# Strassen's seven block products for the second product of a two-layer transformer's MLPs on one Trainium2 core

## The chip, the core and the metric

The kernel runs on one core of a Trainium2 chip. The metric is the device time of one execution in microseconds, as the median of several runs. Five engines matter: TensorE (PE) multiplies matrices, with its weight loads shown apart (PEld); VectorE (DVE) and ScalarE (ACT) do elementwise work and can read the accumulators in PSUM; GpSimd (POOL) does elementwise work on SBUF; SyncE (SP) only issues the DMA loads here. Each engine takes its instructions in the order in which they were issued to it, and they meet at semaphores.

## The reference

Two layers over 256 tokens with a model width of 1024. Layer 0 mixes tokens by block-sparse attention, which with 256 tokens is causal attention over one block; layer 1 by dilated windows. After each mixer comes an MLP with 4096 hidden units:

```python
def sq_relu_mlp(x, w_in, w_out):
    return jnp.square(jax.nn.relu(x @ w_in)) @ w_out

for i in range(DEPTH):
    ...
    h = layer_norm(DEEPNORM_ALPHA * h + mix, ln_mix_g[i], ln_mix_b[i])
    h = layer_norm(DEEPNORM_ALPHA * h + sq_relu_mlp(h, mlp_w_in[i], mlp_w_out[i]),
                   ln_mlp_g[i], ln_mlp_b[i])
```

All is float32. The second product, `... @ w_out`, is 256 x 4096 by 4096 x 1024; it is the one that the change touches.

## The kernel before

**Precision.** PE multiplies in float32r, a rounded form of float32. To keep float32's accuracy each operand is split into a high part (`hi`, rounded) and the rest (`lo`), and a product is three matmuls: hi·hi, hi·lo and lo·hi. ACT makes `hi` with a copy (line 309), DVE makes `lo` by subtracting `hi` from the source (line 314); that pair is `split`. For a weight tile from memory (`load_w`) it is 1024 columns: one load of 512 KB into one of four `raw` buffers, one ACT copy into `whi`, one DVE subtraction into `wlo`, each with ten slots.

**The MLP.** The 4096 hidden units are 32 k-tiles of 128. The first four are computed token-major (`half`, `relu_sq_tok`), with the normalised tokens stationary, since the first half of the tokens is ready before the second; they are then transposed on PE. The other 28 are computed one at a time with a tile of W_in stationary (`mm_wstat_wide`): eight matmuls of 512 columns, which take tokens' hi and lo side by side, and eight of 256 for the weight's lo. `relu_sq_T` takes the result out of its PSUM bank (tag `tp`): an ACT copy of one half, a DVE add of the other, a DVE instruction for relu and square, and a split into `ahi` and `alo`. Four k-tiles after they were made, `do_out` multiplies them by W_out: for each k-tile, two halves of the tokens (m), two halves of the columns (n) and three matmuls, 12 of 512 columns (`mm_rows`, line 318). Four accumulators (tag `acc`) hold the sums; `tp` has four banks, `acc` four, eight in all. The last `TAIL` k-tiles are ordered by accumulator and not by k-tile (`out_and_ln`), so that the first half's normalisation (`ln_half`) starts while the second half still accumulates.

**Order.** All work is first recorded as operations with an engine, an assumed duration and the buffers that they read and write (`Plan.op`). `Plan.order` then simulates the engines with these durations, with slots for each buffer tag, and gives each engine one fixed order by due times; `emit` issues it. An addition on POOL is assumed to take n/480 + 0.17 us (`tt`). POOL has the addition in `rotate` (line 514, 28 times, SBUF to SBUF, 256 elements) and one instruction for each `rstd` of a normalisation (line 699). SP's queue holds all loads in program order.

Of the kernel before, what the change touches and what calls it, by code (L numbers as in the profile page):

```python
# [12 lines left out]
P = 128  # L13
S = 256
# [10 lines left out]
SCALE = HD ** -0.5  # L25
NEG = -1.0e30
BIG = 3.0e38
NCH = DFF // 512
NX = (1, 1)
TAIL = (5, 5, 6, 8)  # L30
NSLOT = 10
ADD_ENG = "POOL"
ORDER0 = (
# [215 lines left out]
def tile_trunk(  # L249
# [42 lines left out]
    def psum(tag):  # L292
        return mk([P, 512], F32, tag, 4, ps_pool)
# [13 lines left out]
    def split(n, src, hi, lo, r, whi, wlo, sbuf=False, hi_eng="ACT"):  # L307
        if hi_eng == "ACT":
            op("ACT", act(n, sbuf=sbuf), lambda: nc.scalar.activation(hi(), src(), AF.Copy), r, whi)  # L309
        else:  # L310
            op("DVE", dve(n), lambda: nc.vector.tensor_copy(hi(), src()), r, whi)
        op(
            "DVE", dve(n),
            lambda: nc.vector.tensor_tensor(lo(), src(), f32(hi()), op=ALU.subtract), list(r) + list(whi), wlo,  # L314
        )

    def mm(out_ap, lhsT, rhs, start, stop):
        nc.tensor.matmul(out_ap, lhsT, rhs, start=start, stop=stop)  # L318
# [115 lines left out]
    def load_gb(i):  # L434
        return load_row(i, lng, "g"), load_row(i, lnb, "b")
# [54 lines left out]
                )  # L490

    def mm_rows(pieces, item, m):
        (ahi, alo, j), w, pos, total = item
        first, last = pos == 0, pos == total - 1
        t = slice(m * P, (m + 1) * P)

        def go():
            a, b = ahi.t[:, j, t], alo.t[:, j, t]
            for acc, c0, n in pieces:
                mm(acc.t[:, :n], a, w.hi.t[:, c0 : c0 + n], first, False)  # L500
                mm(acc.t[:, :n], a, w.lo.t[:, c0 : c0 + n], False, False)
            for acc, c0, n in pieces:
                mm(acc.t[:, :n], b, w.hi.t[:, c0 : c0 + n], False, last)

        op(
            "PE", 3 * sum(n / 2400 + 0.0135 for _, _, n in pieces), go,
            [(w.hi, 0), (w.lo, 0), (ahi, (j, m)), (alo, (j, m))], [acc for acc, _, _ in pieces],
        )
# [7 lines left out]
    def stt(n, aps, dst, a, s, b, o0, o1, r, w):  # L516
        op(
            "DVE", dve(n, aps),
            lambda: nc.vector.scalar_tensor_tensor(dst(), a(), s(), b(), op0=o0, op1=o1), r, w,  # L519
        )  # L520
# [155 lines left out]
    def act_tiles():  # L676
        return mk([P, 4, S], F32R, "ahi", 3), mk([P, 4, S], F32R, "alo", 3)

    def ln_half(pieces, m, gb, last, ahead):
        g, b = gb  # L680
        z = xtok[m]
        step = min(n for _, _, n in pieces)
# [4 lines left out]
        ns = D // step  # L687
        for acc, c0, n in pieces:
            c = slice(c0, c0 + n)
            stt(n, 0, lambda c=c: z.t[:, c], lambda c=c: z.t[:, c], lambda: ALPHA, lambda acc=acc, n=n: acc.t[:, :n],  # L690
                ALU.mult, ALU.add, [(z, c0 // 512), acc] + prev, [(z, c0 // 512)])
            for i in range(c0 // step, (c0 + n) // step):
                op("DVE", dve(step), lambda i=i: nc.vector.bn_stats(st.t[:, i, :], z.t[:, i * step : (i + 1) * step]),  # L693
                   [(z, c0 // 512)], [(st, i)])
                prev = [(st, i)]
# [29 lines left out]
                    [(xs[n], (1, *k)) for k in keys],  # L725
                )

    def new_acc(last=False):
        acc = [[(psum("acc"), n * 512, 512) for n in range(2)] for _ in range(2)]
        if last:  # L730
            acc[1] = [acc[1][0], (acc[1][1][0], 512, 256), (psum("tp"), 768, 256)]
        return acc

    def out_and_ln(acc, items, ntail, gb, last, between):
        k = len(items) - ntail
        for item in items[:k]:
            for m in range(2):
                mm_rows(acc[m], item, m)
        for m in range(2):
            for piece in acc[m]:  # L740
                for item in items[k:]:
                    mm_rows([piece], item, m)
            if m == 1 and between:
                between()
            ln_half(acc[m], m, gb, last, 1.5 if m == 1 and between else 0.0)

    def relu_sq_T(ps, ahi, alo, j):
        u = mk([P, S], F32, "ta", 5)
# [7 lines left out]
            [(ahi, k) for k in keys], [(alo, k) for k in keys], sbuf=True,  # L756
        )

    def relu_sq_tok(ps, m, ahi, alo):
        r = mk([P, 512], F32, "hrt", 1)  # L760
        op("ACT", act(512), lambda: nc.scalar.activation(r.t, ps.t, AF.Relu), [ps], [r])  # L761
        op("ACT", act(512, 0, True), lambda: nc.scalar.activation(r.t, r.t, AF.Square), [r], [r])
        pt = psum("tp")
        transposes(pt, [(j * P, lambda j=j: r.t[:, j * P : (j + 1) * P]) for j in range(4)], [r])
        t = slice(m * P, (m + 1) * P)
        keys = [(j, m) for j in range(4)]
        split(
            512, lambda: pt.t.rearrange("p (j s) -> p j s", j=4), lambda: ahi.t[:, :, t], lambda: alo.t[:, :, t],
            [pt], [(ahi, k) for k in keys], [(alo, k) for k in keys],
        )  # L770

    class Mlp:
        def __init__(self, i, last):
            self.i, self.last = i, last
            self.nx = NX[i]

        def head(self):
            i, nx = self.i, self.nx
            self.ws = [[load_w(win[i][c * 4 + j]) for j in range(4)] for c in range(nx)]
            self.chunks = {c: act_tiles() for c in range(nx)}  # L780
            self.half(0)

        def half(self, m):
            ps = [psum("tp") for _ in range(self.nx)]
            for c in range(self.nx):
                mm_xstat(ps[c], self.ws[c], m, 512, "x")
            for c in range(self.nx):
                relu_sq_tok(ps[c], m, *self.chunks[c])

        def rest(self, between):  # L790
            i, nx, chunks = self.i, self.nx, self.chunks
            self.half(1)
            acc = new_acc(self.last)
            nkt = DFF // P
            ntail = TAIL[2 * i + 1]
            pend = list(range(nx))
            tail = []

            def do_out(c):
                for j in range(4):  # L800
                    pos = c * 4 + j
                    item = ((*chunks[c], j), load_w(wout[i][pos]), pos, nkt)
                    if nkt - pos <= ntail:
                        tail.append(item)
                    else:
                        for m in range(2):
                            mm_rows(acc[m], item, m)

            for c in range(nx, NCH):
                if c == 4:  # L810
                    gb = load_gb(2 * i + 1)
                    if i == 0:
                        ropes.append(const(rope1, [P, 2, S], "ropet"))
                        late["m1"] = const(mask1, [P, 2, 512], "m1")
                chunks[c] = act_tiles()
                for j in range(4):
                    w = load_w(win[i][c * 4 + j])
                    ps = psum("tp")
                    mm_wstat_wide(ps, w)
                    relu_sq_T(ps, *chunks[c], j)  # L820
                pend.append(c)
                while len(pend) > 1:
                    do_out(pend.pop(0))
            while pend:
                do_out(pend.pop(0))
            out_and_ln(acc, tail, len(tail), gb, self.last, between)

    def layer0(between):
        attn = [act_tiles() for _ in range(2)]
# [53 lines left out]
        for step, p in (x.split("-") for x in ORDER0.split()):  # L883
# [13 lines left out]
                sm[p] = softmax(q, k)  # L897
            else:
                pv_causal(*sm.pop(p), V[p // 4], (p % 4) * P, *attn[p // 4], p % 4)
        items = [((*attn[j // 4], j % 4), load_w(wo0[j]), j, 8) for j in range(8)]  # L900
# [18 lines left out]
    def layer1(between):  # L919
# [4 lines left out]
        for step, a in (x.split("-") for x in ORDER1.split()):  # L924
# [49 lines left out]
            else:  # L974
# [8 lines left out]
        items = [((*attn[j // 3], j % 3), load_w(wo1[j]), j, 6) for j in range(6)]  # L983
        out_and_ln(new_acc(), items, TAIL[2], gb, False, between)

    mlps = [Mlp(0, False), Mlp(1, True)]
# [14 lines left out]
def _layout(inputs):  # L1001
# [34 lines left out]
    wi = []  # L1036
    for i in range(DEPTH):
        t = a["mlp_w_in"][i]
        k = NX[i] * 512
        parts = ([wide_tiles(t[:, :k], 512)] if k else []) + [col_tiles(t[:, k:])]  # L1040
        wi.append(np.concatenate(parts))
# [57 lines left out]
```

## Time and profile before

| | us |
|---|---|
| median of 3 runs (577.32 to 578.2) | 577.36 |
| profiled execution | 577.73 |
| its span | 576.0 |
| MLP of layer 0 with its neighbours, stretch 135 to 310 | 175 |
| MLP of layer 1, stretch 395 to 560 | 165 |
| DMA in all | 105.61 MB, 183 GB/s over the span |

The span goes from the first to the last instruction that the profiler recorded, the time from start to end of the execution. Busy shares count an engine's instructions from start to end. Matmuls overlap in a pipeline, so their mean duration (379 ns for 512 columns) is longer than the step from one to the next; steps are read from the chain or from counts in a stretch. An instruction that waits within the engine for something shows as a longer one and not as idle time.

### The profile page before, as it was taken

How to read it: one execution, taken by the hardware profiler on the slowest of the kernel's cores; microseconds unless marked ns; L12 is line 12 of the kernel's file. 1: busy time of each engine (PE TensorE's matmuls, PEld its weight loads, DVE VectorE, ACT ScalarE, POOL GpSimd, SP SyncE). 2: the span in 40 equal slices, each digit the busy share in tenths (PEclk: the TensorE clock that was granted, in tenths of full speed). 3: DMA queues.
4: the chain of work that ended last, by engine and by line, in shares of the span. 5: the costliest groups of instructions: out<-in, count | busy, mean ns of one | idle time of the engine just before them, and what ended most of it. 6: DMA issues, size and time to landing. Idle time of an engine off the chain costs nothing.

```text
span 576.0 us, 8655 instructions
## 1 busy us (share of the span) xinstructions
PE 563.0 (98%) x3234; PEld 486.9 (85%) x3234; DVE 430.1 (75%) x771; ACT 300.5 (52%) x501; POOL 40.4 (7%) x41
## 2 busy tenths in 40 slices
PE   8899999999999999999999999999999999999994
PEld 7799898788888888888888999878888888888884
DVE  5799989798874775665768899978876756756544
ACT  6585677636753554454525455754764544544400
POOL 0211121010000000000000323000000000000000
PEclk9899999999999999999999999999999999999998
DMA  8644943726986875565524533544888655655101
GB/s 303 236 151 151 326 130 123 221 74 220 304 261 220 258 215 185 184 205 181 197 75 158 207 112 111 172 157 129 279 279 263 202 196 172 200 184 182 36 1 73
DMA packets 30281, 105.61 MB, mean 183 GB/s; under 512 B 3488, under 2 KB 4256, under 8 KB 30240
## 3 DMA queue, kind: packets, MB, share of 16 engines
q1 hardware_dynamic: 30240, 105.07, 56.0%
q8 instruction: 25, 0.41, 0.3%
q14 instruction: 16, 0.13, 0.1%
HBM read 104.01 MB, written 1.05 MB: 182 GB/s over the span
## 4 chain that ended last, share of the span: by engine, by line
PE 95%; DVE 1%; DMA 1%; ACT 1%; issue 0%; POOL 0%; SPq 0%; DVEq 0%
PE acc L318 55%; PE tp L318 38%; PE tp L598 2%; DMA raw<-in_xw_dram 1%; DVE ta L512 0%; DVE tok L519 0%; POOL ta L514 0%; ACT xs L309 0%; ACT hrt L761 0%; DVE wlo L314 0%; SPq L305 0%; ACT whi L309 0%; ACT khi L540 0%; DVE klo L519 0%; DVE bst L693 0%
## 5 line engine op out<-in xcount | busy, mean ns | idle before, releaser
L314 DVE TENSOR_TENSOR wlo<-raw,whi 128x1024 fp32r<-128x1024 f32 (+2 forms) x185 | 225.6, 1226 | 74.1 <-ACT whi L309 73.0
L309 ACT ACTIVATE whi<-raw 128x1024 fp32r<-128x1024 f32 (+2 forms) x184 | 191.3, 1046 | 129.6 <-PE tp L318 57.1
L318 PE MATMUL acc<-whi,ahi 128*128 128x512 f32 (+1 forms) x312 | 119.6, 383 | 0.0
L318 PE MATMUL acc<-wlo,ahi 128*128 128x512 f32 (+1 forms) x312 | 117.3, 380 | 0.0
L318 PE MATMUL tp<-xs,whi 128*128 128x512 f32 x448 | 112.0, 392 | 0.0
L318 PE MATMUL acc<-whi,alo 128*128 128x512 f32 (+1 forms) x312 | 100.7, 379 | 0.0
L318 PEld LDWEIGHTS tp<-xs,whi 128*128 128x128 f32 x448 | 81.1, 189 | 14.9
L318 PEld LDWEIGHTS acc<-whi,ahi 128*128 128x128 f32 x312 | 58.7, 188 | 11.3 <-issue 0.9
L318 PEld LDWEIGHTS acc<-wlo,ahi 128*128 128x128 f32 x312 | 58.7, 188 | 10.4
L318 PE MATMUL acc<-xs,whi 128*128 128x256 f32 x448 | 64.9, 288 | 1.5 <-ACT whi L309 1.5
L318 PEld LDWEIGHTS acc<-whi,alo 128*128 128x128 f32 x312 | 57.1, 188 | 10.4
L318 PEld LDWEIGHTS tp<-xs,wlo 128*128 128x128 f32 x448 | 61.0, 190 | 4.2
L318 PE MATMUL tp<-xs,wlo 128*128 128x256 f32 x448 | 62.6, 283 | 0.0
L318 PEld LDWEIGHTS acc<-xs,whi 128*128 128x128 f32 x448 | 58.6, 192 | 4.2 <-issue 1.8
L512 DVE TENSOR_TENSOR ta<-acc,ropet 64x256 f32<-64x256 f32 (+1 forms) x84 | 35.3, 421 | 7.5 <-PE acc L318 6.4
L514 POOL TENSOR_TENSOR ta<-ta,ta 128x256 f32<-128x256 f32 x28 | 31.7, 1137 | 117.1 <-DVE ta L512 112.6
L309 ACT ACTIVATE ahi<-ta 128x256 fp32r<-128x256 f32 x56 | 23.0, 410 | 28.3 <-DVE ta L519 28.1
L699 POOL TENSOR_TENSOR rstd<-rstd,expo 128x1 f32<-128x1 f32 x8 | 7.9, 988 | 412.5 <-DVE rstd L697 412.5
L318 PE MATMUL acc<-xs,wlo 128*128 128x256 f32 x224 | 34.7, 284 | 0.0
L512 DVE TENSOR_TENSOR ta<-tp,ta 128x256 f32<-128x256 f32 x56 | 23.4, 418 | 14.0 <-ACT ta L751 14.0
L751 ACT ACTIVATE ta<-tp 128x256 f32<-128x256 f32 x56 | 21.0, 375 | 20.3 <-PE tp L318 20.2
L318 PE MATMUL acc<-whi,xs 128*128 128x512 f32 (+1 forms) x112 | 29.5, 371 | 1.8 <-DVE ta L512 1.8
(83 smaller groups left out, 553.7 us busy)
## 6 DMA issues: line engine op xcount, KB each, us to landing
raw<-in_win_dram SPq DMA_DIRECT2D x64, 512.0 KB, 4.4
raw<-in_wout_dram SPq DMA_DIRECT2D x64, 512.0 KB, 4.2
raw<-in_wqk_dram SPq DMA_DIRECT2D x24, 512.0 KB, 3.7
raw<-in_wo_dram SPq DMA_DIRECT2D x14, 512.0 KB, 3.3
raw<-in_wv_dram SPq DMA_DIRECT2D x8, 512.0 KB, 5.5
g<-in_lng_dram SPq DMA_DIRECT2D x4, 512.0 KB, 5.3
b<-in_lnb_dram SPq DMA_DIRECT2D x4, 512.0 KB, 7.5
raw<-in_wv1a_dram SPq DMA_DIRECT2D x4, 512.0 KB, 3.2
```

Of the source, the lines that this page charges most:

```text
L309: op("ACT", act(n, sbuf=sbuf), lambda: nc.scalar.activation(hi(), src(), AF.Copy), r, whi)
L314: lambda: nc.vector.tensor_tensor(lo(), src(), f32(hi()), op=ALU.subtract), list(r) + list(whi), wlo,
L318: nc.tensor.matmul(out_ap, lhsT, rhs, start=start, stop=stop)
L512: op("DVE", dve(n) + extra, lambda: nc.vector.tensor_tensor(out_ap(), a(), b(), op=alu), r, w)
L514: op("POOL", n / 480 + 0.17, lambda: nc.gpsimd.tensor_tensor(out_ap(), a(), b(), op=alu), r, w)
L598: nc.tensor.transpose(ps.t[:, c : c + P], src(), ident.t)
L699: op("POOL", 0.98, lambda: nc.gpsimd.tensor_tensor(rs.t[:, 1:2], rs.t[:, 0:1], expo.t, op=ALU.pow), [(rs, 0), expo], [(rs, 1)])
L751: op("ACT", act(S), lambda: nc.scalar.activation(u.t, ps.t[:, S:], AF.Copy), [ps], [u])
```

## The change

For a pair of k-tiles the second product is a product of 2 x 2 blocks: A has two token halves by two k-tiles (128 x 128 each), B two k-tiles by two column halves (128 x 512 each). By rows and columns that is eight block products of three matmuls. The changed kernel uses Strassen's algorithm in Winograd's form for the first 13 pairs of each layer: seven block products, four sums of blocks of A, four of B. The last three pairs (six k-tiles) are multiplied as before.

- `Pair` takes the activations of a pair. Its blocks lie in `x`, POOL makes the four sums of 128 columns in `s`, and the blocks that are needed are split in 384 and 512 columns. The square is done by ACT in place of DVE.
- `PairW` loads two k-tiles of W_out, POOL makes four differences of 512 columns (in the buffers `sc0`, `sc1`, `pt0`, `pt1` of the attention), and ACT and DVE split 512 + 1024 columns of loaded blocks and four times 512 of differences, 3584 columns in place of 2048.
- `product` is one block product, three matmuls of 512 columns into its own bank. Each of the seven products accumulates over all 13 pairs, in seven of the eight PSUM banks. One bank, `tp`, is left for the results of the first product.
- After the last pair eleven DVE instructions of 512 columns add the finished products to the residual `xtok`; three banks go on as accumulators of the last six k-tiles, together with one that comes free.
- In layer 1 the last accumulator was cut into 512 + 256 + 256 columns for all k-tiles; now for the last six only. `TAIL` goes from 5 and 8 k-tiles in the two MLPs to 6 and 6.
- The loads of g, b, the mask and the rotation table of layer 1 move from one place to four, after k-tiles 14, 18, 22 and 24.

```diff
-TAIL = (5, 5, 6, 8)
+TAIL = (5, 5, 6, 6)
+NPAIR = (13, 13)
...
+    class Pair:
+        def __init__(self):
+            self.x, self.s = mk([P, 512], F32, "v", 4), mk([P, 512], F32, "v", 4)
+            self.hi, self.lo = act_tiles()
+        def split(self):
+            x, s = self.x, self.s
+            for i, (a, b, alu) in enumerate((
+                ((x, 3), (x, 2), ALU.add), ((s, 0), (x, 0), ALU.subtract), ((x, 0), (x, 3), ALU.subtract),
+                ((x, 1), (s, 1), ALU.subtract),
+            )):
+                tt(
+                    P, lambda i=i: blocks(s.t)[:, i], lambda a=a: blocks(a[0].t)[:, a[1]],
+                    lambda b=b: blocks(b[0].t)[:, b[1]], alu, [a, b], [(s, i)], "POOL",
+                )
+            for src, c0, n in ((x, 0, 3), (s, 3, 4)):
...
+                split(
+                    n * P, lambda src=src, n=n: src.t[:, : n * P], lambda flat=flat: flat(self.hi),
+                    lambda flat=flat: flat(self.lo), [(src, i) for i in range(n)],
+                    [(self.hi, k) for k in keys], [(self.lo, k) for k in keys], sbuf=True,
+                )
+        def fill(self, ps, j):
+            x = self.x
+            u = mk([P, S], F32, "ta", 5)
+            op("ACT", act(S), lambda: nc.scalar.activation(u.t, ps.t[:, S:], AF.Copy), [ps], [u])
+            tt(S, lambda: u.t, lambda: ps.t[:, :S], lambda: u.t, ALU.add, [ps, u], [u])
+            op("ACT", act(S, 0, True), lambda: nc.scalar.activation(u.t, u.t, AF.Relu), [u], [u])
...
+    class PairW:
+        def __init__(self, src):
+            raw = []
+            for i in range(2):
+                r = mk([P, 1024], F32, "raw", 4)
+                dma(lambda r=r, i=i: r.t, src[i], (), [(r, 0)], P * 4096)
+                raw.append(r)
...
+            t = [mk([P, 512], F32, tag, n) for tag, n in (("sc0", 3), ("sc1", 3), ("pt0", 2), ("pt1", 2))]
...
+            self.put(raw[0], 0, 512, ["11"], 0)
+            for i, a, b in ((1, "12", "11"), (3, "22", "12"), (2, "22", "t1"), (4, "21", "t2")):
+                d, x, y = w[f"t{i}"], w[a], w[b]
+                tt(
+                    512, lambda d=d: d[0].t[:, d[1]], lambda x=x: x[0].t[:, x[1]], lambda y=y: y[0].t[:, y[1]],
+                    ALU.subtract, [(x[0], x[2]), (y[0], y[2])], [d[0]], "POOL",
+                )
+            self.put(raw[1], 0, 1024, ["21", "22"], 0)
+            for a, b in ((1, 3), (2, 4)):
+                home = None
+                for i in (a, b):
+                    home = self.put(t[i - 1], 512 * (i == b), 512, [f"t{i}"], None, home)
...
+    def product(ps, i, pair, w, first, last):
+        x, name = SEVEN[i]
+        hi, lo, c, key = w.at[name]
+        def go():
+            a, b = (t.t.rearrange("p a b -> p (a b)")[:, x * P : (x + 1) * P] for t in (pair.hi, pair.lo))
+            mm(ps.t, a, hi.t[:, c], first, False)
+            mm(ps.t, a, lo.t[:, c], False, False)
+            mm(ps.t, b, hi.t[:, c], False, last)
+        op("PE", 3 * 0.2296, go, [(hi, key), (lo, key), (pair.hi, x), (pair.lo, x)], [ps])
...
+            banks = {j: psum("acc") for j in (0, 1, 2, 3)}
+            banks.update({j: psum("tp") for j in (4, 5, 6)})
+            outs = [(p, js) for p in range(npair) for js in ((0, 1, 3, 4), (6, 5, 2))]
...
+            for k in range(4, nkt):
+                if outs:
+                    do_out(*outs.pop(0))
...
+                do_in(k)
+            while outs:
+                do_out(*outs.pop(0))
+            for m, n, j in (
+                (0, 0, 0), (0, 1, 0), (1, 0, 0), (1, 1, 0), (0, 1, 5), (1, 0, 5), (1, 1, 5), (1, 0, 6), (1, 1, 6),
+                (0, 1, 4), (1, 1, 4),
+            ):
+                z, c, ps = xtok[m], slice(n * 512, (n + 1) * 512), banks[j]
+                stt(
+                    512, 0, lambda z=z, c=c: z.t[:, c], lambda z=z, c=c: z.t[:, c],
+                    lambda j=j: ALPHA if j == 0 else 1.0, lambda ps=ps: ps.t, ALU.mult, ALU.add, [(z, n), ps], [(z, n)],
+                )
+            acc = [[(banks[1], 0, 512), (banks[2], 512, 512)], [(banks[3], 0, 512)]]
```

More of the change, by code (lines that the diff above doesn't have):

```diff
@@ L27 @@
 BIG = 3.0e38
-NCH = DFF // 512
-NX = (1, 1)
-TAIL = (5, 5, 6, 8)
+TAIL = (5, 5, 6, 6)
+NPAIR = (13, 13)
 NSLOT = 10
@@ L492, in mm_rows @@
     def mm_rows(pieces, item, m):
-        (ahi, alo, j), w, pos, total = item
+        (ahi, alo, j), w, pos, total, begun = item
         first, last = pos == 0, pos == total - 1
@@ L499, in go @@
             for acc, c0, n in pieces:
-                mm(acc.t[:, :n], a, w.hi.t[:, c0 : c0 + n], first, False)
+                mm(acc.t[:, :n], a, w.hi.t[:, c0 : c0 + n], first and acc not in begun, False)
                 mm(acc.t[:, :n], a, w.lo.t[:, c0 : c0 + n], False, False)
@@ L677, in act_tiles, with ln_half @@
         return mk([P, 4, S], F32R, "ahi", 3), mk([P, 4, S], F32R, "alo", 3)
-    def ln_half(pieces, m, gb, last, ahead):
+    def ln_half(pieces, m, gb, last, ahead, alpha=ALPHA):
         g, b = gb
@@ L689, in ln_half @@
             c = slice(c0, c0 + n)
-            stt(n, 0, lambda c=c: z.t[:, c], lambda c=c: z.t[:, c], lambda: ALPHA, lambda acc=acc, n=n: acc.t[:, :n],
+            stt(n, 0, lambda c=c: z.t[:, c], lambda c=c: z.t[:, c], lambda: alpha, lambda acc=acc, n=n: acc.t[:, :n],
                 ALU.mult, ALU.add, [(z, c0 // 512), acc] + prev, [(z, c0 // 512)])
@@ L726, in ln_half, with new_acc, out_and_ln @@
                 )
[L728 to L734, printed above, removed]
+    def new_acc():
+        return [[(psum("acc"), n * 512, 512) for n in range(2)] for _ in range(2)]
+    def out_and_ln(acc, items, ntail, gb, last, between, alpha=ALPHA):
         k = len(items) - ntail
@@ L744, in out_and_ln @@
                 between()
-            ln_half(acc[m], m, gb, last, 1.5 if m == 1 and between else 0.0)
+            ln_half(acc[m], m, gb, last, 1.5 if m == 1 and between else 0.0, alpha)
     def relu_sq_T(ps, ahi, alo, j):
@@ L757, in relu_sq_T, with blocks, relu_sq_tok @@
         )
-    def relu_sq_tok(ps, m, ahi, alo):
+    def blocks(t):
+        return t.rearrange("p (b s) -> p b s", s=P)
+    class Pair:
[13 more added lines that the diff above has]
+            for src, c0, n in ((x, 0, 3), (s, 3, 4)):
+                c = slice(c0 * P, (c0 + n) * P)
+                flat = lambda t, c=c: t.t.rearrange("p a b -> p (a b)")[:, c]
+                keys = [c0 + i for i in range(n)]
+                split(
[9 more added lines that the diff above has]
+            op("ACT", act(S, 0, True), lambda: nc.scalar.activation(u.t, u.t, AF.Relu), [u], [u])
+            keys = ((0, 3), (1, 2))[j]
+            op(
+                "ACT", act(S, 0, True),
+                lambda: nc.scalar.activation(
+                    blocks(x.t)[:, keys[0] : keys[1] + 1 : keys[1] - keys[0]], blocks(u.t), AF.Square
+                ),
+                [u], [(x, k) for k in keys],
+            )
+    def relu_sq_tok(ps, m, pairs):
         r = mk([P, 512], F32, "hrt", 1)
@@ L763, in relu_sq_tok @@
         pt = psum("tp")
[L764 to L770, printed above, removed]
+        order = (1, 0, 3, 2) if m else (0, 1, 2, 3)
+        transposes(pt, [(i * P, lambda j=j: r.t[:, j * P : (j + 1) * P]) for i, j in enumerate(order)], [r])
@@ new lines, in relu_sq_tok, with put @@
+        for q, pair in enumerate(pairs):
+            op(
+                "ACT", act(S),
+                lambda q=q, pair=pair: nc.scalar.activation(
+                    pair.x.t[:, m * S : (m + 1) * S], pt.t[:, q * S : (q + 1) * S], AF.Copy
+                ),
+                [pt], [(pair.x, 2 * m), (pair.x, 2 * m + 1)],
+            )
[6 more added lines that the diff above has]
+                raw.append(r)
+            half = (slice(0, 512), slice(512, 1024))
+            self.at = {}
+            t = [mk([P, 512], F32, tag, n) for tag, n in (("sc0", 3), ("sc1", 3), ("pt0", 2), ("pt1", 2))]
+            w = {n: (raw[i], half[j], 0) for n, i, j in (("11", 0, 0), ("12", 0, 1), ("21", 1, 0), ("22", 1, 1))}
+            w.update({f"t{i + 1}": (t[i], half[0], None) for i in range(4)})
+            self.put(raw[0], 0, 512, ["11"], 0)
[4 more added lines that the diff above has]
+                    ALU.subtract, [(x[0], x[2]), (y[0], y[2])], [d[0]], "POOL",
+                )
+            self.put(raw[1], 0, 1024, ["21", "22"], 0)
[3 more added lines that the diff above has]
+                    home = self.put(t[i - 1], 512 * (i == b), 512, [f"t{i}"], None, home)
+        def put(self, src, c0, n, names, key, home=None):
+            hi, lo = home or [mk([P, 1024], F32R, tag, NSLOT) for tag in ("whi", "wlo")]
+            c = slice(c0, c0 + n)
+            split(
+                n, lambda: src.t[:, :n], lambda: hi.t[:, c], lambda: lo.t[:, c], [(src, key)], [(hi, c0)],
+                [(lo, c0)], sbuf=True,
+            )
+            for i, name in enumerate(names):
+                self.at[name] = (hi, lo, slice(c0 + 512 * i, c0 + 512 * i + 512), c0)
+            return hi, lo
@@ new lines, in tile_trunk @@
+    SEVEN = ((0, "11"), (1, "21"), (6, "22"), (2, "t4"), (3, "t1"), (4, "t2"), (5, "t3"))
+    def product(ps, i, pair, w, first, last):
[7 more added lines that the diff above has]
+        op("PE", 3 * 0.2296, go, [(hi, key), (lo, key), (pair.hi, x), (pair.lo, x)], [ps])
@@ L774, in __init__ @@
             self.i, self.last = i, last
-            self.nx = NX[i]
         def head(self):
-            i, nx = self.i, self.nx
-            self.ws = [[load_w(win[i][c * 4 + j]) for j in range(4)] for c in range(nx)]
-            self.chunks = {c: act_tiles() for c in range(nx)}
+            self.ws = [load_w(win[self.i][j]) for j in range(4)]
+            self.pairs = [Pair() for _ in range(2)]
             self.half(0)
         def half(self, m):
-            ps = [psum("tp") for _ in range(self.nx)]
@@ L785, in half @@
[L785 to L788, printed above, removed]
+            ps = psum("tp")
+            mm_xstat(ps, self.ws, m, 512, "x")
+            relu_sq_tok(ps, m, self.pairs)
         def rest(self, between):
-            i, nx, chunks = self.i, self.nx, self.chunks
+            i, pairs = self.i, self.pairs
             self.half(1)
-            acc = new_acc(self.last)
@@ L794, in rest @@
[L794 to L823, printed above, removed]
@@ L824, in rest, with do_in @@
-            while pend:
-                do_out(pend.pop(0))
-            out_and_ln(acc, tail, len(tail), gb, self.last, between)
+            for pair in pairs:
+                pair.split()
+            nkt, npair = DFF // P, NPAIR[i]
+            banks = {j: psum("acc") for j in (0, 1, 2, 3)}
+            banks.update({j: psum("tp") for j in (4, 5, 6)})
+            outs = [(p, js) for p in range(npair) for js in ((0, 1, 3, 4), (6, 5, 2))]
+            rows = {}
+            pw = {}
+            def do_in(k):
+                w = load_w(win[i][k])
+                ps = psum("tp")
+                mm_wstat_wide(ps, w)
+                if k // 2 < npair:
+                    if k % 2 == 0:
+                        pairs.append(Pair())
+                    pairs[k // 2].fill(ps, k % 2)
+                    if k % 2:
+                        pairs[k // 2].split()
+                else:
+                    if not rows or k % 4 == 0:
+                        self.tiles = act_tiles()
+                    rows[k] = (*self.tiles, k % 4)
+                    relu_sq_T(ps, *rows[k])
@@ new lines, in do_out @@
+            def do_out(p, js):
+                if p not in pw:
+                    pw[p] = PairW([wout[i][2 * p + j] for j in range(2)])
+                for j in js:
+                    product(banks[j], j, pairs[p], pw[p], p == 0, p == npair - 1 and j in (0, 4, 5, 6))
+            for k in range(4, nkt):
+                if outs:
+                    do_out(*outs.pop(0))
+                if k == 14:
+                    gb = [load_row(2 * i + 1, lng, "g")]
+                elif k == 18:
+                    gb.append(load_row(2 * i + 1, lnb, "b"))
+                elif k == 22 and i == 0:
+                    late["m1"] = const(mask1, [P, 2, 512], "m1")
+                elif k == 24 and i == 0:
+                    ropes.append(const(rope1, [P, 2, S], "ropet"))
+                do_in(k)
@@ new lines, in rest @@
+            while outs:
[8 more added lines that the diff above has]
+                    lambda j=j: ALPHA if j == 0 else 1.0, lambda ps=ps: ps.t, ALU.mult, ALU.add, [(z, n), ps], [(z, n)],
+                )
@@ L828, in layer0 @@
+            acc = [[(banks[1], 0, 512), (banks[2], 512, 512)], [(banks[3], 0, 512)]]
+            acc[1] += [(psum("acc"), 512, 256), (psum("tp"), 768, 256)] if self.last else [(psum("acc"), 512, 512)]
+            ks = list(range(2 * npair, nkt))
+            begun = tuple(banks[j] for j in (1, 2, 3))
+            items = [(rows[k], load_w(wout[i][k]), n, len(ks), begun) for n, k in enumerate(ks)]
+            out_and_ln(acc, items, TAIL[2 * i + 1], gb, self.last, between, 1.0)
     def layer0(between):
@@ L899, in layer0 @@
                 pv_causal(*sm.pop(p), V[p // 4], (p % 4) * P, *attn[p // 4], p % 4)
-        items = [((*attn[j // 4], j % 4), load_w(wo0[j]), j, 8) for j in range(8)]
+        items = [((*attn[j // 4], j % 4), load_w(wo0[j]), j, 8, ()) for j in range(8)]
         out_and_ln(new_acc(), items, TAIL[0], (late["g"], late["b"]), False, between)
@@ L982, in layer1 @@
                     pv_diag(e, P + gi * P, r, v, vc, *attn[u], gi)
-        items = [((*attn[j // 3], j % 3), load_w(wo1[j]), j, 6) for j in range(6)]
+        items = [((*attn[j // 3], j % 3), load_w(wo1[j]), j, 6, ()) for j in range(6)]
         out_and_ln(new_acc(), items, TAIL[2], gb, False, between)
@@ L1038, in _layout @@
         t = a["mlp_w_in"][i]
-        k = NX[i] * 512
-        parts = ([wide_tiles(t[:, :k], 512)] if k else []) + [col_tiles(t[:, k:])]
-        wi.append(np.concatenate(parts))
+        wi.append(np.concatenate([wide_tiles(t[:, :512], 512), col_tiles(t[:, 512:])]))
     d["win"] = np.stack(wi)
```

## The prediction

> **What bounds the kernel now.** I read the page first (span, busy shares, the chain that ended last), then the chain in order of time for the two MLPs, then busy time by stretches, then the groups of instructions by form, and last the order of time around the few instructions that POOL has.
>
> ```profile
> span 576.0 us, 8655 instructions
> PE 563.0 (98%) x3234; PEld 486.9 (85%) x3234; DVE 430.1 (75%) x771; ACT 300.5 (52%) x501; POOL 40.4 (7%) x41
> PE 95%; DVE 1%; DMA 1%; ACT 1%; issue 0%; POOL 0%; SPq 0%; DVEq 0%
> ```
>
> TensorE is the bound: 95% of the chain is PE, and it is busy for 563 of 576.0 us. The profiled execution took 577.73 us, 1.7 us more than its span; the median of the runs is 577.36 us, so the sum below starts from 577.7 and stands 0.4 us above the median.
>
> ```profile
> 158.87 11.15 PE tp L318 x64
> 170.01 10.91 PE acc L318 x48
> ...
> 135.00:310.00 175.00, 175.00 (x887) 149.16 (x886) 121.44 (x174) 90.28 (x129) 1.98 (x2) 1.00 0.63 205
> 395.00:560.00 165.00, 165.00 (x901) 143.07 (x901) 108.41 (x155) 80.30 (x118) 0.70 (x1) 1.00 0.58 185
> ```
>
> The first two rows are the rhythm of an MLP in the chain: four tiles of the first product (64 matmuls, 11.15 us, 2.79 us a tile), then four k-tiles of the second (48 matmuls, 10.91 us, 0.2273 us a matmul, 2.73 us a k-tile). The stretches (columns: span, PE, PE weight load, DVE, ACT, POOL, clock, DMA share, GB/s) show PE without a gap, DVE at 121 of 175 us, ACT at 90, POOL at 2. So a matmul saved in the MLP is time saved, as long as the others keep up. DVE has 54 us of slack in 175; POOL looks empty.
>
> **What the change removes.** 26 pairs of k-tiles (13 a layer) need 21 matmuls of 512 columns in place of 24. That is 78 fewer: 78 x 0.2273 = 17.7 us of PE. A pair with its two tiles of the first product then costs PE 2 x 2.79 + 21 x 0.2273 = 10.35 us. That is the pace the other engines must keep.
>
> **What it adds, per pair.** On DVE, by these rows:
>
> ```profile
> L314 DVE TENSOR_TENSOR wlo<-raw,whi 128x1024 fp32r<-128x1024 f32 x180 | 222.7, 1244 | 73.7 <-ACT whi L309 73.0
> L314 DVE TENSOR_TENSOR wlo<-tok,whi 128x512 fp32r<-128x512 f32 x2 | 1.4, 688 | 0.0
> L314 DVE TENSOR_TENSOR alo<-ta,ahi 128x256 fp32r<-128x256 f32 x56 | 23.5, 420 | 6.8 <-ACT ahi L309 6.5
> L512 DVE TENSOR_TENSOR ta<-tp,ta 128x256 f32<-128x256 f32 x56 | 23.4, 418 | 14.0 <-ACT ta L751 14.0
> L519 DVE SCALAR_TENSOR_TENSOR ta<-ta 128x256 f32<-128x256 f32 x56 | 23.7, 423 | 1.3
> L519 DVE SCALAR_TENSOR_TENSOR tok<-tok,acc 128x512 f32<-128x512 f32 x15 | 10.3, 684 | 15.7 <-PE acc L318 15.5
> ```
>
> Three splits of 1024 (two tiles of W_in and the raw half of W_out that goes in whole): 3.73 us. Five of 512 (one raw block, four sums): 3.44. The activations in 384 (between 420 and 688 ns, 0.55) and 512 (0.69). Two adds out of PSUM, 0.84. Together 9.25 us. The square moves from DVE to ACT, so two of the 423 ns instructions leave. By itself DVE fits under 10.35 us, barely.
>
> On POOL there are eight subtractions and additions a pair, four on 512 elements and four on 128, all SBUF to SBUF. The trace has only the 256-element add of the rotation, alone and beside DVE:
>
> ```profile
> 39.19 0.74 POOL L514 TENSOR_TENSOR ta<-ta,ta 128x256 f32<-128x256 f32 x1 [8.87 <-DVE ta L512]
> 39.42 0.42 DVE L574 CUSTOM_DVE_ANT_0 sc<-tp,m 128x256 f32<-128x256 f32 x1
> ...
> 41.77 0.89 POOL L514 TENSOR_TENSOR ta<-ta,ta 128x256 f32<-128x256 f32 x1 [1.85 <-DVE ta L512]
> 42.01 1.75 DVE L314 TENSOR_TENSOR wlo<-raw,whi 128x1024 fp32r<-128x1024 f32 x1
> ...
> 92.89 1.23 DVE L314 TENSOR_TENSOR wlo<-raw,whi 128x1024 fp32r<-128x1024 f32 x1
> 93.00 1.71 POOL L514 TENSOR_TENSOR ta<-ta,ta 128x256 f32<-128x256 f32 x1 [6.32 <-DVE ta L512]
> 94.03 1.29 DVE L512 TENSOR_TENSOR ta<-acc,ropet 128x256 f32<-128x256 f32 x3
> ```
>
> This is the view that decides. Beside a DVE instruction that reads PSUM (39.42) the add takes 0.74 us and neither is longer for it. Beside a DVE split, whose two inputs both lie in SBUF, the two take turns. At 41.77 POOL is first: it ends at 42.66, and the split, 1.23 us elsewhere, takes 1.75 and ends at 43.76, 1.10 us after POOL. At 92.89 DVE is first: it ends at 94.12, and POOL takes 1.71 and ends at 94.71, 0.59 us after. So a POOL add and a DVE split with two SBUF inputs do not run at once; only about 0.13 us of each start hides under the other. POOL's time is not free: it is taken from DVE.
>
> [...]
>
> Price of POOL: beside DVE a 256-element add costs 0.59 us. For 512 elements the bounds are 0.59 (no dearer than 256) and 1.48 (twice the whole 0.74); I take 1.18, in proportion. For 128: 0.30, half (between about nothing and 0.74). Eight: 4 x 1.18 + 4 x 0.30 = 5.92 us a pair.
>
> [...] No run here shows these sizes yet.
>
> **The sum.** A pair in steady state: 9.25 (DVE) + 5.92 (POOL) - 8 x 0.13 (starts hidden at the eight handoffs) = 14.1 us; the two PSUM adds may run beside POOL, which makes 13.3. I take 13.7, against PE's 10.35. Now one layer:
> - 11 pairs with their two first-product tiles: 11 x 13.7 = 150.7.
> - The first two pairs, whose activations come from the token-major head: 9.25 - 2.49 - 0.84 + 5.92 - 1.04 = 10.8 each, 21.6; POOL's four weight sums of the first (4.7) stand in its order before the last normalisation's second rstd, so they are done before: 16.9.
> - Three 1024 splits for the plain k-tiles that stand in DVE's order before the last pair's last split: 3.7.
> - Then PE ends the layer: the last half pair 3 x 0.68 = 2.0, four first-product tiles 11.2, six plain k-tiles 16.4: 29.6. DVE's work left beside it (nine 1024 splits, 18 of 256, eleven 684 ns additions of the block products: 11.2 + 7.6 + 7.5 = 26.3) fits under that.
>
> 201 us. Before, the same work is PE's 28 x 2.79 + 32 x 2.73 = 165.5. Plus 35.5 a layer, 71 for two, with PE's 17.7 already in it (without the gain in matmuls nothing here would be shorter, since DVE and POOL set the pace): 577.7 + 71 = 649, say **650 us**.
>
> **Costed at nothing.** ACT has a pair's 3 x 1.06 + 5 x 0.63 of weights, 2 x (0.38 + 0.41 + 0.41) of the evacuation and 0.52 + 0.63 of the activations, 9.9 us:
>
> ```profile
> L309 ACT ACTIVATE whi<-raw 128x1024 fp32r<-128x1024 f32 x180 | 188.9, 1056 | 129.5 <-PE tp L318 57.1 <-PE acc L318 47.3 <-DMA raw<-in_win_dram 9.8
> L309 ACT ACTIVATE whi<-tok 128x512 fp32r<-128x512 f32 x2 | 1.3, 633 | 0.0
> L309 ACT ACTIVATE whi<-raw 128x384 fp32r<-128x384 f32 x1 | 0.5, 523 | 0.0
> L309 ACT ACTIVATE ahi<-ta 128x256 fp32r<-128x256 f32 x56 | 23.0, 410 | 28.3 <-DVE ta L519 28.1
> L751 ACT ACTIVATE ta<-tp 128x256 f32<-128x256 f32 x56 | 21.0, 375 | 20.3 <-PE tp L318 20.2
> L699 POOL TENSOR_TENSOR rstd<-rstd,expo 128x1 f32<-128x1 f32 x8 | 7.9, 988 | 412.5 <-DVE rstd L697 412.5
> ```
>
> It hides under 13.7; at PE's pace of 10.35 it would be the next bound. The first rstd of a normalisation (988 ns) now stands on POOL behind two weight sums that wait for their loads; PE has the second half's tail meanwhile, and without that cover it costs about 2 us a layer. The loads keep their bytes; g, b, mask and rope loads are only spread out on SP's queue, which the chain of waits shows at 0%. A raw buffer of W_out is now held until four POOL sums are done: 4.2 us of load plus some 9 us twice, and about 4.4 + 3 us twice for W_in, over four buffers is about 10.3 us a pair, below 13.7. At PE's pace it would bind.
>
> **Rivals.**
> 1. The turns are dearer (0.20). POOL's sums wait for each other, DVE's splits wait for POOL by way of ACT, all three run in an order fixed beforehand without these turns. If no start hides, POOL scales from 0.74 (7.40) and nothing runs beside it, a pair is 9.25 + 7.40 = 16.65 us: 183.2 + 20.7 + 3.7 + 29.6 = 237 a layer, 721 us. [...] For it: each of a pair's four weight sums passes from POOL to ACT to DVE. [...]
> 2. POOL is cheap for its size (0.10). At 0.59 for 512 too, POOL is 3.56 a pair, 11.3 us with the rest: 124.3 + 14.4 + 3.7 + 29.6 = 172, 591 us. Against: only one size is in the trace.
> 3. Faster (0.09): the overlap holds where queues are long, DVE and POOL both stay under 10.35, PE stays the bound, 577.7 - 17.7 = 560 us. It decides as soon as DVE plus POOL fall below 10.35 a pair, which needs POOL's part below about 2.1 us; 3.56 is already the low bound of rows. The two overlapped pairs above speak against it.
> 4. The one spare PSUM bank (0.05). Seven of eight banks hold products, so every first-product tile waits until the one before is out of its bank. Here is such an evacuation:
>
> ```profile
> 205.84 0.39 ACT L751 ACTIVATE ta<-tp 128x256 f32<-128x256 f32 x1
> 205.92 1.23 DVE L314 TENSOR_TENSOR wlo<-raw,whi 128x1024 fp32r<-128x1024 f32 x1 [0.59 <-ACT whi L309]
> 207.06 0.42 DVE L512 TENSOR_TENSOR ta<-tp,ta 128x256 f32<-128x256 f32 x1
> ```
>
> It takes 1.64 us, with DVE's add behind one split; three or four products (2.05 or 2.73 us) lie between. With one more 1.23 us split ahead 0.8 us shows: 56 x 0.8 - 17.7 = +27, 605 us without the turns. Within the forecast it hides.
>
> The change does what it says: 104 sums of 512 and 104 of 128 stand on POOL, so that it has no effect isn't among the cases.
>
> **How the numbers follow.** Forecast 0.56, with its own range of 625 to 685 (a pair at 12.6 to 15.3 us). Rivals 0.20, 0.10, 0.09, 0.05. From 600 to 720 leaves out rival 3, half of rival 2 and a little of rival 1, about 2 in 10. A measurement here tells 0.2% (1.2 us) from no change. Faster: rival 3 less the strip about no change, 0.08; same 0.02; slower 0.90.
>
> **What would show it.** In the MLP stretches: DVE instructions with two SBUF inputs and POOL's sums abutting, splits of 512 well over 0.69 us (about 1.2 to 1.9), PE busy about 75 to 80%, waiting mostly for DVE's low parts; POOL's 512-element sum alone at about 1.3 us. A pair should recur every 13 to 15 us. The attention stretches stay as they are. Wrong if PE stays above 95% busy in an MLP, if splits keep 0.69 and 1.24 us beside POOL, or if PE waits for loads or for the spare bank instead.

## The result and the profile after

| | before, us | after, us |
|---|---|---|
| median of 4 runs | 577.34 | 650.1 |
| range | 577.09 to 578.2 | 649.86 to 650.42 |
| span of the profiled execution | 576.0 | 648.6 |

The changed kernel takes 1.126 times as long (95% interval 1.124 to 1.128). As its diff shows, `TAIL` is 5 and 6 k-tiles in its two MLPs, and not 6 and 6 as said above; no number below depends on it.

The page of the changed kernel: its span, busy times, and the chain's shares by engine.

```profile
span 648.6 us, 8937 instructions
...
PE 572.9 (88%) x3078; PEld 478.6 (74%) x3078; DVE 582.3 (90%) x857; ACT 384.5 (59%) x705; POOL 310.1 (48%) x249
...
PE 39%; DVE 23%; POOL 15%; issue 12%; ACT 7%; DMA 3%; DVEq 0%; SPq 0%; POOLq 0%; ACTq 0%
```

PE has fewer matmuls and is no longer the chain: 39% against 95%. DVE went from 430 to 582 us of busy time with 86 instructions more, POOL from 40 to 310. Both counts hold time in which an instruction waits for the other engine, which the groups by form show:

```profile
L314 DVE TENSOR_TENSOR wlo<-raw,whi 128x1024 fp32r<-128x1024 f32 x154 | 225.9, 1473 | 4.0 <-ACT whi L309 3.7
L314 DVE TENSOR_TENSOR wlo<-sc,whi 128x512 fp32r<-128x512 f32 x52 | 54.9, 1064 | 0.2 <-ACT whi L309 0.2
L314 DVE TENSOR_TENSOR wlo<-pt,whi 128x512 fp32r<-128x512 f32 x52 | 45.3, 881 | 0.6 <-ACT whi L309 0.6
L314 DVE TENSOR_TENSOR wlo<-raw,whi 128x512 fp32r<-128x512 f32 x29 | 35.9, 1238 | 0.4 <-ACT whi L309 0.3
...
L512 DVE TENSOR_TENSOR ta<-tp,ta 128x256 f32<-128x256 f32 x56 | 23.0, 414 | 7.1 <-ACT ta L791 5.3 <-ACT ta L748 1.2
```

Splits with two SBUF inputs grew from 1244 to 1473 ns and from 688 to 881, 1064 and 1238 ns. The add out of PSUM in the same stretch stayed at 414 (418 before). Only instructions that read two SBUF tensors are longer; no other form of DVE's grew by more than 2 ns.

Here is a piece of a pair, in order of time (start, duration, engine, line):

```profile
224.04 2.26 POOL L514 TENSOR_TENSOR pt<-raw,raw 128x512 f32<-128x512 f32 x1
225.09 0.41 DVE L512 TENSOR_TENSOR ta<-tp,ta 128x256 f32<-128x256 f32 x1
225.42 1.43 DVE L314 TENSOR_TENSOR wlo<-sc,whi 128x512 fp32r<-128x512 f32 x1
...
226.27 1.74 POOL L514 TENSOR_TENSOR pt<-raw,sc 128x512 f32<-128x512 f32 x1
...
227.01 1.55 DVE L314 TENSOR_TENSOR wlo<-pt,whi 128x512 fp32r<-128x512 f32 x1 [0.15 <-ACT whi L309]
```

The PSUM add at 225.09 runs in the middle of POOL's sum. The split at 225.42 takes 1.43 in place of 0.69 us: POOL ends at 226.30, the split at 226.85, 0.55 us later. POOL's next sum ends at 228.01, 1.16 us after that split; the split at 227.01 ends at 228.56, 0.55 after POOL. They alternate.

The first weight sum of the fourth and of the thirteenth pair of layer 0, on POOL:

```profile
163.06 2.21 POOL L514 TENSOR_TENSOR sc<-raw 128x512 f32<-128x512 f32 x1 [1.20 <-DVE wlo L314]
...
285.72 1.30 POOL L514 TENSOR_TENSOR sc<-raw 128x512 f32<-128x512 f32 x1
```

Nine pairs in 122.66 us: 13.6 us a pair. Busy time in such a stretch, for the changed kernel (span, PE, PE weight load, DVE, ACT, POOL, clock, DMA share, GB/s), and what PE waits for in the whole execution (us, times, longest):

```profile
163.00:298.00 135.00, 112.32 (x519) 90.77 (x518) 124.68 (x122) 86.47 (x158) 101.70 (x80) 0.94 0.51 172
```

```profile
PE tp L318 <- DVE ta L512: 51.4, 34, 4.1
PE acc L318 <- DVE alo L314: 4.6, 2, 3.6
```

DVE is occupied for 92% of the stretch, PE for 83%. PE stands still mainly before a first-product tile, for the add that empties the one spare bank. That add itself takes 0.41 us; it stands in DVE's order behind splits that POOL's sums have made longer. Without this lengthening PE hardly waits for it: 6.5 us in the run without sums below.

Where the loss lies (72.7 us by the last of these rows, 72.8 by the medians) can be read from POOL's instruction for the second half's normalisation, four times in each kernel. Before:

```profile
126.40 0.99 POOL L699 TENSOR_TENSOR rstd<-rstd,expo 128x1 f32<-128x1 f32 x1 [6.97 <-DVE rstd L697]
...
304.92 0.99 POOL L699 TENSOR_TENSOR rstd<-rstd,expo 128x1 f32<-128x1 f32 x1 [6.70 <-DVE rstd L697]
...
391.07 0.99 POOL L699 TENSOR_TENSOR rstd<-rstd,expo 128x1 f32<-128x1 f32 x1 [5.63 <-DVE rstd L697]
...
570.02 0.98 POOL L699 TENSOR_TENSOR rstd<-rstd,expo 128x1 f32<-128x1 f32 x1 [9.74 <-DVE rstd L697]
```

After:

```profile
127.43 0.99 POOL L699 TENSOR_TENSOR rstd<-rstd,expo 128x1 f32<-128x1 f32 x1 [5.01 <-DVE rstd L697]
...
339.42 0.99 POOL L699 TENSOR_TENSOR rstd<-rstd,expo 128x1 f32<-128x1 f32 x1 [6.74 <-DVE rstd L697]
...
429.92 0.99 POOL L699 TENSOR_TENSOR rstd<-rstd,expo 128x1 f32<-128x1 f32 x1 [5.61 <-DVE rstd L697]
...
642.72 0.99 POOL L699 TENSOR_TENSOR rstd<-rstd,expo 128x1 f32<-128x1 f32 x1 [6.93 <-DVE rstd L697]
```

The MLP of layer 0 went from 178.5 to 212.0 us (+33.5), that of layer 1 from 179.0 to 212.8 (+33.8). The rest are the stretches before the MLPs, +1.0 and +4.3 (86.2 to 90.5).

### The profile page after: what moved, and what is told of

Its sections match the earlier page's. It is cut to its first block, busy times and chain, and to the rows that moved or that the text cites. A ratio compares the mean times of both kernels' runs of the same rounds, so it can differ in the third digit from the quotient of the medians.

```text
span 648.6 us, 8937 instructions
## 1 busy us (share of the span) xinstructions
PE 572.9 (88%) x3078; PEld 478.6 (74%) x3078; DVE 582.3 (90%) x857; ACT 384.5 (59%) x705; POOL 310.1 (48%) x249
## 3 DMA queue, kind: packets, MB, share of 16 engines
HBM read 104.01 MB, written 1.05 MB: 162 GB/s over the span
## 4 chain that ended last, share of the span: by engine, by line
PE 39%; DVE 23%; POOL 15%; issue 12%; ACT 7%; DMA 3%; DVEq 0%; SPq 0%; POOLq 0%; ACTq 0%
PE acc L318 22%; PE tp L318 15%; DVE wlo L314 14%; POOL v L514 9%; DVE ta L512 4%; POOL pt L514 3%; ACT whi L309 2%; POOL sc L514 2%; DVE tok L519 2%; DMA raw<-in_wout_dram 2%; PE tp L598 2%; DVE alo L314 1%; ACT ahi L309 1%; ACT ta L793 1%; ACT v L797 1%
## 5 line engine op out<-in xcount | busy, mean ns | idle before, releaser
L314 DVE TENSOR_TENSOR wlo<-raw,whi 128x1024 fp32r<-128x1024 f32 (+2 forms) x185 | 259.3, 1425 | 4.5 <-ACT whi L309 4.0
L318 PEld LDWEIGHTS tp<-xs,whi 128*128 128x128 f32 x448 | 85.2, 198 | 86.2 <-DVE ta L512 63.0
L318 PE MATMUL acc<-whi,ahi 128*128 128x512 f32 (+1 forms) x208 | 83.5, 401 | 0.0
L318 PE MATMUL acc<-wlo,ahi 128*128 128x512 f32 (+1 forms) x208 | 82.1, 394 | 0.0
L514 POOL TENSOR_TENSOR v<-v 128x128 f32<-128x128 f32 x52 | 50.2, 971 | 62.8 <-ACT v L797 62.8
L314 DVE TENSOR_TENSOR alo<-v,ahi 128x384 fp32r<-128x384 f32 (+1 forms) x52 | 49.7, 956 | 19.1 <-ACT ahi L309 18.7
L514 POOL TENSOR_TENSOR sc<-raw 128x512 f32<-128x512 f32 x26 | 40.1, 1543 | 52.1 <-DMA raw<-in_wout_dram 50.9
L314 DVE TENSOR_TENSOR wlo<-sc,whi 128x512 fp32r<-128x512 f32 x52 | 54.9, 1064 | 0.2 <-ACT whi L309 0.2
L514 POOL TENSOR_TENSOR pt<-raw,raw 128x512 f32<-128x512 f32 x26 | 54.9, 2110 | 0.0
L309 ACT ACTIVATE ahi<-v 128x384 fp32r<-128x384 f32 (+1 forms) x52 | 29.9, 575 | 33.5 <-POOL v L514 33.1
L314 DVE TENSOR_TENSOR wlo<-pt,whi 128x512 fp32r<-128x512 f32 x52 | 45.3, 881 | 0.6 <-ACT whi L309 0.6
```

Source lines behind the costliest of these rows:

```text
L514: op("POOL", n / 480 + 0.17, lambda: nc.gpsimd.tensor_tensor(out_ap(), a(), b(), op=alu), r, w)
```

## The experiments

The theory: POOL's sums and DVE's splits exclude each other because both read SBUF, so that the sums' time is added to DVE's and passes PE's. The rivals: the chain of waits from POOL over ACT to DVE; the one spare PSUM bank; PE itself. All runs are of one core, each beside runs of the kernel before on the same chip (577.5 and 577.3 us).

**The sums on DVE.**

```diff
-                    lambda b=b: blocks(b[0].t)[:, b[1]], alu, [a, b], [(s, i)], "POOL",
+                    lambda b=b: blocks(b[0].t)[:, b[1]], alu, [a, b], [(s, i)],
...
-                    ALU.subtract, [(x[0], x[2]), (y[0], y[2])], [d[0]], "POOL",
+                    ALU.subtract, [(x[0], x[2]), (y[0], y[2])], [d[0]],
```

> All 208 block sums go from POOL to DVE, nothing else changes. Theory (DVE and POOL take turns, so POOL's sums are paid in DVE's time): a pair costs 9.25 us of DVE plus four sums of 512 at 0.69 and four of 128 at about 0.29, 13.1 us in place of 13.7; 630 to 640 us. Rival (POOL works beside DVE, the loss has another cause): 3.9 us more DVE work a pair, 26 times, on top of 650: about 750 us.

Measured: 631.0 us, 1.093 times before (1.091 to 1.095). Splits of 512 and the first sum of five successive pairs on DVE, groups by form and then in order of time:

```profile
L314 DVE TENSOR_TENSOR wlo<-sc,whi 128x512 fp32r<-128x512 f32 x52 | 35.6, 684 | 0.0
```

```profile
203.43 0.68 DVE L512 TENSOR_TENSOR sc<-raw 128x512 f32<-128x512 f32 x1
...
255.53 0.69 DVE L512 TENSOR_TENSOR sc<-raw 128x512 f32<-128x512 f32 x1
```

The splits are back at 684 ns, and a pair takes 52.1 / 4 = 13.0 us (13.1 expected). An engine given all of the other's work is 19 us faster than the two together: the POOL offload was worse than none.

**The sums made but not read.** POOL works as before; splits take loaded blocks in place of the sums.

```diff
-            for src, c0, n in ((x, 0, 3), (s, 3, 4)):
+            for src, c0, n in ((x, 0, 3), (x, 3, 4)):
...
-                    home = self.put(t[i - 1], 512 * (i == b), 512, [f"t{i}"], None, home)
+                    home = self.put(raw[i // 3], 512 * (i == b), 512, [f"t{i}"], 0, home)
```

> POOL makes the same sums, but no split reads them: ACT and DVE split loaded blocks of the same size instead, so nobody waits for POOL (the result is not the reference's: the sums are left out of the products). Theory (turns): DVE and POOL still exclude each other, 635 to 655 us. Rival (the time is lost in the chain of waits POOL to ACT to DVE): 570 to 600 us.

Measured: 654.3 us, 1.133 times before (1.131 to 1.135). DVE and POOL by form:

```profile
L314 DVE TENSOR_TENSOR wlo<-raw,whi 128x512 fp32r<-128x512 f32 x133 | 143.7, 1113 | 2.9 <-ACT whi L309 2.6
```

```profile
L514 POOL TENSOR_TENSOR pt<-raw,raw 128x512 f32<-128x512 f32 x26 | 54.4, 2094 | 0.0
```

Neither ACT, DVE nor PE waits for a sum, POOL's share of the chain falls from 15% to 1%, and nothing is won: splits of 512 take 1113 ns. So the chain of waits from POOL over ACT to DVE is not what costs the time. The 654 us need not be turns alone, though: a loaded block is held until its last split here, and the next run and the last show what that can cost.

**No sums.** As the last, with the sums taken out.

```diff
-            for i, a, b in ((1, "12", "11"), (3, "22", "12"), (2, "22", "t1"), (4, "21", "t2")):
-                d, x, y = w[f"t{i}"], w[a], w[b]
-                tt(
...
```

> No sums at all; PE, ACT and DVE do as many instructions of the same sizes as in the changed kernel, and splits read loaded blocks (the sums are left out of the result). Theory (turns): DVE's 9.25 us a pair lie under PE's 10.35 again, 560 to 575 us. Rival (one spare PSUM bank, or ACT, or DVE alone is the bound): 600 us or more.

Measured: 577.0 us, 0.999 times before (0.998 to 1.000). All of the 73 us lost came back, but not the 17.7 that PE saves. That is 2 us above the expected range and well under the rival's 600. The six-buffer run below takes this up.

**POOL writes, but does not read.** Each sum becomes memsets of the same block. The waits of ACT and DVE for POOL's blocks stay.

```diff
-                tt(
-                    512, lambda d=d: d[0].t[:, d[1]], lambda x=x: x[0].t[:, x[1]], lambda y=y: y[0].t[:, y[1]],
-                    ALU.subtract, [(x[0], x[2]), (y[0], y[2])], [d[0]], "POOL",
+                op(
+                    "POOL", 512 / 480 + 0.17,
+                    lambda d=d: [nc.gpsimd.memset(d[0].t[:, d[1]], 0.01) for _ in range(NFILL)],
+                    [(x[0], x[2]), (y[0], y[2])], [d[0]],
                 )
```

> Each sum on POOL is replaced by two memsets of the same block, so POOL writes but reads nothing; ACT and DVE still wait for POOL's blocks and split them (the sums are left out of the result). Theory (DVE's second SBUF input and POOL's reads exclude each other): the exclusion goes, the waits stay, 560 to 585 us. Rival (waits): 630 us or more. If POOL's writes exclude DVE as well, it stays above 600 with splits of 512 well over 0.69 us.

> As e4_pool_writes_only, with three memsets for each sum in place of two: POOL is then busy for longer (about 1.6 us a block of 512) than a sum takes it alone (1.3 us). Theory (only POOL's reads exclude DVE's second input): 558 to 566 us. Rival (e4 was fast because POOL had less to do): 575 us or more.

Measured: 560.6 us with two memsets (0.971 times before, 0.969 to 0.973), 561.2 us with three (0.972, 0.969 to 0.975). With two, DVE and then POOL, by form:

```profile
L315 DVE TENSOR_TENSOR wlo<-sc,whi 128x512 fp32r<-128x512 f32 x52 | 35.1, 684 | 0.0
```

```profile
L839 POOL MEMSET sc<- 128x512 f32 x104 | 53.8, 527 | 6.3 <-PE tp L599 3.3
```

With three there are half as many again, 1.58 us a block, longer than a sum alone (1.30):

```profile
L839 POOL MEMSET sc<- 128x512 f32 x156 | 81.2, 527 | 9.3 <-PE tp L599 3.3
```

This is the decisive pair. With three memsets POOL is busy for longer than the sums take it alone, ACT and DVE still come behind its blocks in the order, and 28 first-product tiles a layer still go through the one spare bank. Yet the kernel runs at PE's pace, 16 to 17 us under the kernel before, and with two memsets PE's 51.4 us of waiting for the add are gone: first-product tiles have no such wait of over 0.5 us in sum, and PE is busy for 155.0 of 155 us in each of the two MLP stretches (135 to 290 and 390 to 545). What the 650 us need is POOL's reading: beside sums, which read two blocks, a split of a POOL block takes 881 to 1064 ns on average, and beside memsets, which read none, 684 to 687. A POOL instruction that reads one block only was not tried.

**Weight sums twice.**

```diff
+                for _ in range(2):
                     tt(
                         512, lambda d=d: d[0].t[:, d[1]], lambda x=x: x[0].t[:, x[1]], lambda y=y: y[0].t[:, y[1]],
```

> Each of the 104 weight sums of 512 is made twice on POOL, one after the other into the same block. Theory (turns): every sum beside DVE costs the pair 1.18 us more, 104 x 1.18 = 123: 760 to 785 us. Rival (POOL has idle time, since it is busy for 48% of the span with its waiting counted, and the loss is elsewhere): 650 to 690 us.

Measured: 753.1 us, 1.305 times before (1.299 to 1.311). 104 more sums cost 103 us, 0.99 each. That is under the expected range by 7 us. The expectation took 1.18 us a sum and left out the hidden start of 0.13 us that the prediction's sum takes off for each; with it a sum is 1.05 us and the time 759 us. A sum of 512 is thus dearer in this stage than the 0.69 us that DVE would take for it. It costs 0.31 us less than the 1.30 it takes alone, so POOL's idle share gave little room.

**More work for PE.** Each block product issues its third matmul twice.

```diff
+            mm(ps.t, b, hi.t[:, c], False, False)
             mm(ps.t, b, hi.t[:, c], False, last)
```

> Each block product issues its third matmul twice: 7 more matmuls a pair, 182 in all (the low part of the activations is counted twice in the result). Theory (DVE and POOL set the pace at 13.6 us a pair, PE needs 10.35 and now 11.9): 645 to 665 us. Rival (PE still sets the pace between waits, as its 39% of the chain may be read): 182 x 0.2273 = 41 us more, 691 us.

Measured: 653.3 us, 1.132 times before (1.129 to 1.135), 3.2 us above the changed kernel for 41 us of matmuls. Its stretch:

```profile
163.00:298.00 135.00, 124.34 (x599) 101.25 (x598) 127.51 (x121) 87.68 (x159) 102.22 (x80) 0.99 0.51 171
```

PE is busier by 12 us there, and the whole execution hardly longer. So what Strassen's algorithm took off PE was taken off an engine that now waits.

**No sums, with six raw buffers.**

```diff
-NSLOT = 10
+NSLOT = 9
...
-                r = mk([P, 1024], F32, "raw", 4)
+                r = mk([P, 1024], F32, "raw", 6)
```

> As e3_no_sums (no sums; splits read loaded blocks, so a loaded block is held until its last split), with six raw buffers in place of four and nine slots for split weights in place of ten. The 16 us between e3 (577.0) and e4 (560.6) have two readings. Theory (loads wait for raw buffers at PE's pace, as the prediction put under costed at nothing): 560 to 567 us. Rival (the spare PSUM bank or the changed order): 574 us or more.

Measured: 559.7 us, 0.970 times before (0.967 to 0.972). In the run with four buffers the chain in order of time has loads in it:

```profile
502.30 6.45 DMA raw<-in_wout_dram
525.18 7.49 DMA raw<-in_win_dram
```

With four, ACT waits for loads of W_in and W_out for 3.7 and 3.5 us; with six, neither is among its waits. So the 17 us that were missing without sums came from loads waiting for a buffer, since there a block is held until its last split. The spare bank costs nothing visible by itself at PE's pace: 559.7 us is PE's saving whole (577.3 - 17.7 = 559.6).

## Why the prediction was right

- **What bounds the kernel after.** Right. It is DVE and POOL in turns, shown by three kernels together: sums made and read (650), sums made and unread (654, with loaded blocks held longer), blocks written without reading (561).
- **PE's saving of 17.7 us.** Right in size (559.7 to 561.2 us once DVE and POOL do not collide), and worth nothing in the changed kernel, where even 182 matmuls more cost 3 us.
- **The pace of 13.7 us a pair.** Measured 13.6, with two errors that cancel. In the stretch above DVE was busy for 12.6 us a pair (124.68 us in 9.9 pairs), where its instructions alone would take 9.25 by the prediction's rows. POOL's sums made them longer by some 3.3 us a pair; the sum had 4.45 (13.7 - 9.25). Against that DVE was idle for 1.0 us a pair, which the sum had at nothing. By the waits of that stretch about half of the idle time is for ACT's copy of a first-product tile (5.3 us of 10.3) and most of the rest for ACT's high parts (4.8). So a little of the first rival, the waits between queues, is real. A weight sum was sized about right: 1.18 less one hidden start is 1.05, and 0.99 was measured. Why the sums together cost less than in the prediction was not taken apart.
- **35.5 us a layer.** Measured 33.5 and 33.8, 3.7 too much in two layers. The normalisations before the MLPs were costed at nothing, with 2 us a layer if cover was missing; they took 1.0 and 4.3. About half of the 4.3 is the same turn. Two DVE instructions of the second normalisation, before:

```profile
385.61 1.41 DVE L519 SCALAR_TENSOR_TENSOR tok<-tok,rstd,b 128x512 f32<-128x512 f32 x2
```

and after, beside POOL's last two sums for the first pair:

```profile
421.19 1.44 POOL L514 TENSOR_TENSOR pt<-raw,sc 128x512 f32<-128x512 f32 x1
421.39 3.47 DVE L519 SCALAR_TENSOR_TENSOR tok<-tok,rstd,b 128x512 f32<-128x512 f32 x2
422.59 1.73 POOL L514 TENSOR_TENSOR pt<-raw,raw 128x512 f32<-128x512 f32 x1
```

1.41 us became 3.47, which is 2.1 of the 4.3 us. With POOL only writing (two memsets) the same stretch took 88.5 us (from 295.77 to 384.25), so that 2.3 us over the 86.2 of before do not come from POOL's reading; their cause stays open. I counted these sums as done for nothing before the stage. That 650 was met to a fraction of a microsecond is thus partly luck: +5.3 us left out and 3.7 us too much, and the rest of it rounding.

- **The rivals.** The turns dearer (721): fell, since it needed 16.65 us a pair, and 13.6 was measured. POOL cheap for its size (591): fell, by the 0.99 us. The spare bank: fell as a cause, though PE's waits (51 us) are recorded there; with POOL only writing they are gone through the same bank. Faster (560): fell, and it is exactly what the kernel does when POOL stops reading.
- **Signs.** Splits of 512 at 0.88 to 1.24 us on average were less long than the 1.2 to 1.9 foretold. PE at 83% was above 75 to 80%; its matmuls were longer (those of 512 columns in the first product 421 ns on average in place of 392), and its clock was lower (below). PE was to wait for DVE's low parts; it waits for the add behind them. POOL's sum of 512 alone is 1.30 us, as said.

## What to carry to other kernels

In this kernel two-input work on POOL was paid for in DVE's time (12.6 us a pair in place of 9.25). Before such work goes to POOL, add its time for two-input SBUF operations to the time of all DVE instructions in that stage that read two SBUF tensors: the sum, not each by itself, has to fit under the engine that bounds the stage. If it does not, the same operation on DVE is cheaper (0.69 against 0.99 us for 512 elements here), and what goes to POOL should read nothing (splits of 512 stayed at 684 to 687 ns beside memsets) or run beside DVE work that reads PSUM (adds stayed at 414 ns). No version here that makes Strassen's sums and uses them beat the kernel before: the sums on DVE need 13.0 us a pair against PE's 10.35; mixing pairs among plain k-tiles, where DVE has room, was not tried.

## What was not expected of the hardware

PE's granted clock was 1.00 in the MLP of layer 0 before and 0.94 in the stretch after, though PE was busy for 83% of it and its longest wait there was 2.9 us. What lowers it stays open. With the extra matmuls it was 0.99, at nearly the same time, which speaks against the clock as the cause of the loss. And the waiting fell on some DVE instructions and not on others: DVE's adds out of PSUM stayed at 414 ns, one of them in the middle of a POOL sum, while the split with two SBUF inputs right behind it took 1.43 us in place of 0.69 and ended 0.55 us after POOL.
